# Expert rows fetched by indirect DMA and transposed, in place of one-hot products; gate and up weights in 4 KB runs

## The chip, the cores and the metric

One Trainium2 chip, one core of it. The metric is the device time of one execution of the whole program, in microseconds; lower is better.

## What is computed

The program is two layers behind each other on 512 tokens of width 1024, all in float32. The change lies in the expert part of the first layer, a mixture of 32 experts with 256 hidden columns each:

```python
h2 = rmsnorm(x, norm_ffn_g).reshape(b * s, d)
m = hierarchical_moe(h2, ...)
return x + m.reshape(b, s, d)

# hierarchical_moe, h is 512 x 1024
g_sel = argmax(group_logits)                       # one of 8 groups per token
top_vals, top_idx = lax.top_k(in_group, 2)         # two of the group's 4 experts
w_top = jax.nn.softmax(top_vals, axis=-1) * w_grp
combine = sum(one_hot(g_sel * 4 + top_idx, 32) * w_top[..., None], axis=1)
for e in range(32):
    hid = jax.nn.silu(h @ w_gate[e]) * (h @ w_up[e])   # 1024 -> 256
    out = out + (hid @ w_down[e]) * combine[:, e:e + 1]
```

Each token thus goes through two experts. The second layer (a convolution branch, a recurrent branch and a feed-forward part) is not touched.

## The kernel before

The whole first layer keeps its 512 rows `x` on the chip as 8 tiles of 128 x 512 (four blocks of 128 tokens, two halves of the width). Ahead of the experts, VectorE computes the routing from small logits (L763 to L841): per token and expert a position `pos` in the expert's list, and the combine weight `Cw`. An expert has 64 slots (`_CAP`); should any have more tokens, a loop under `tc.If(nmax > _CAP)` (L934) does the rest. With these inputs it is skipped.

The experts are worked off in 8 quads of four, and a quad in 2 pairs of two experts, so that a pair has 2 x 64 = 128 slots, one partition each. The order is:

- `onehots(qd)` (L811): VectorE compares slot numbers with `pos`: one 128 x 256 one-hot per block of tokens, slots of the quad's four experts along the columns.
- `gather(qd, oh)` (L858): the rows of a quad by products with the one-hots. Ahead of it, ScalarE and POOL or VectorE have split x into a rounded half `h2h` and a rest `h2l` (`halve`, L742 and L743). For each of 8 blocks of 128 features, four blocks of tokens times two halves are summed in PSUM: 64 matmuls of 128 x 256 (L867, L868). ScalarE (L870) and VectorE (L871) take the results out and scale them by the norm's gain. The result `xg` is already turned: features on partitions, slots along the columns.
- `pair(pr_, XG)` (L875): two 32-row products with a selector spread the positions and the weights over slots (L883, L887, L888); VectorE makes `oht` (L885), the one-hot with slots on partitions, and by two reductions (L890, L891) the scales `cw`. Then 64 matmuls with gate and up weights (L897), `Silu` on ScalarE (L900), the product with up and weight on VectorE (L901), two transposes (L904), their evacuation (`hT`, L153 or L155), 16 matmuls with the down weights (L912), and `split_t` of the result into halves `yph` (ScalarE, L159) and `ypl` (VectorE, L160).
- scatter, after both pairs of a quad: for each block of tokens and half of the width four matmuls with `oht` (L1021, L1022) and an addition to x (L1023). It is written under `tc.high_priority(offset=-200)`, which lets the scheduler put these 32 matmuls between the instructions of the next quad.

Weights come by `wexp` and `load_pair` (L719, L732) on SyncE's queue (L728): 12 tiles of 512 KB per pair, into a ring of 20 tiles (`NWE`). A tile of gate or up holds four blocks of 128 rows, row k x 128 + p on partition p, so each partition reads four runs of 256 numbers (1 KB); a down tile is one run of 1024 numbers (4 KB) per partition. The meta tokens of the second layer are prepared between the routing and the first quad (L999 to L1009); the tile `pmt` for their transposes is a PSUM tile of the tag `ms`.

The tile framework decides the order on each engine and the waits; every engine then works its list in order. PSUM tags have so many buffers: `xg` 1, `pg` 2, `py` 2, `ms` 1, `cb` 2. The scatter and its additions use `cb`; `oht`, `hd` and `hT` are tiles of the tag `T`.

The loop and the sizes that matter:

```python
PS.update({"xg": 1, "pg": 2, "py": 2, "ms": 1, "cb": 2})
for qd in range(8):
    XG = gather(qd, onehots(qd) if qd else oh0)
    YP = [pair(2 * qd + i, XG) for i in range(2)]
    with tc.high_priority(offset=-200):
        ...
```

## Time and profile before

| what | value |
|---|---|
| median of 3 runs | 2106.84 us (2103.09 to 2111.01) |
| the profiled execution | 2107.09 us, of it 2105.2 us in the span of the trace |
| mean granted TensorE clock | 0.987 of full speed |
| busy in the span | TensorE 96%, VectorE 64%, ScalarE 40%, POOL 1% |
| moved by DMA | 236.66 MB, 112 GB/s on average |

The expert stage lies at about 500 to 865 us of the span. A row of the trace names a line of the kernel, an engine, an operation and its tiles, output first. `PEld` is TensorE's load of the stationary operand, which overlaps the matmuls; `SPq` is SyncE's DMA queue. A line in a helper (L153, L155, L159, L160) stands for all that call it, so the tile's name tells which it is. In rows of the tables by stretch, `PEclk` is the granted clock as a share of full speed. A matmul's end is modelled, and consecutive matmuls overlap in the array.

### The profile page before, as it was taken

How to read it: one execution, taken by the hardware profiler on the slowest of the kernel's cores; microseconds unless marked ns; L12 is line 12 of the kernel's file. 1: busy time of each engine (PE TensorE's matmuls, PEld its weight loads, DVE VectorE, ACT ScalarE, POOL GpSimd, SP SyncE). 2: the span in 40 equal slices, each digit the busy share in tenths (PEclk: the TensorE clock that was granted, in tenths of full speed). 3: DMA queues.
4: the chain of work that ended last, by engine and by line, in shares of the span. 5: the costliest groups of instructions: out<-in, count | busy, mean ns of one | idle time of the engine just before them, and what ended most of it. 6: DMA issues, size and time to landing. Idle time of an engine off the chain costs nothing.

```text
span 2105.2 us, 42119 instructions
## 1 busy us (share of the span) xinstructions
PE 2018.8 (96%) x17517; PEld 1716.4 (82%) x17517; DVE 1340.9 (64%) x2937; ACT 842.2 (40%) x1741; POOL 23.9 (1%) x89
## 2 busy tenths in 40 slices
PE   7999999997999999899999999989999999999998
PEld 7778587886666666699888888878799989899997
DVE  4799835444434433879999889986443476455566
ACT  5443634332111111756655656544433253233333
POOL 0000000000000000100000000000000000000000
PEclk9999999998999999999999999989999999999999
DMA  5112021372799987321122212113443323332331
GB/s 159 56 31 82 21 80 41 100 258 68 251 313 326 307 289 253 53 79 54 40 57 57 56 42 57 53 42 102 151 124 97 107 61 92 97 93 90 91 116 51
DMA packets 282390, 236.66 MB, mean 112 GB/s; under 512 B 31500, under 2 KB 255795, under 8 KB 282195
## 3 DMA queue, kind: packets, MB, share of 16 engines
q1 hardware_dynamic: 282195, 233.92, 36.5%
q8 instruction: 140, 2.29, 0.5%
q14 instruction: 55, 0.45, 0.1%
HBM read 225.14 MB, written 8.74 MB: 111 GB/s over the span
## 4 chain that ended last, share of the span: by engine, by line
PE 61%; DVE 8%; ACT 4%; issue 1%; DMA 1%; SPq 0%; DVEq 0%; ACTq 0%
PE m L193 10%; PE m L191 10%; PE m L192 10%; PE ps L897 6%; PE ps L912 3%; DVE cv L1583 3%; PE ps L867 2%; PE q L191 2%; PE q L193 2%; PE q L192 2%; PE ps L868 1%; PE ps L1021 1%; PE ps L1022 1%; PE y L1522 1%; DVE wl L160 1%; PE x L1419 1%
## 5 line engine op out<-in xcount | busy, mean ns | idle before, releaser
L191 PE MATMUL m<-hh,wh 128*128 128x258 f32 (+1 forms) x1648 | 468.9, 290 | 7.9 <-ACT wh L159 3.0
L193 PE MATMUL m<-hh,wl 128*128 128x258 f32 (+1 forms) x1648 | 466.6, 290 | 3.4 <-DVE wl L160 2.1
L192 PE MATMUL m<-hl,wh 128*128 128x258 f32 (+1 forms) x1648 | 466.4, 289 | 2.4 <-DVE hl L160 1.7
L160 DVE TENSOR_TENSOR wl<-wr,wh 128x1024 fp32r<-128x1024 f32 (+1 forms) x205 | 248.0, 1212 | 227.7 <-ACT wh L159 224.7
L159 ACT ACTIVATE wh<-wr 128x1024 fp32r<-128x1024 f32 (+1 forms) x205 | 214.9, 1050 | 374.7 <-PE m L192 220.3
L191 PEld LDWEIGHTS m<-hh,wh 128*128 128x128 f32 x1648 | 308.3, 189 | 14.3 <-ACT wh L159 3.8
L193 PEld LDWEIGHTS m<-hh,wl 128*128 128x128 f32 x1648 | 307.7, 189 | 8.5 <-DVE wl L160 3.4
L192 PEld LDWEIGHTS m<-hl,wh 128*128 128x128 f32 x1648 | 308.5, 189 | 6.9 <-DVE hl L160 2.3
L1583 DVE SCALAR_TENSOR_TENSOR cv<-th,vec,cv 128x516 f32<-128x516 f32 (+9 forms) x240 | 176.5, 738 | 2.6
L897 PE MATMUL ps<-we,xg 128*64 128x256 f32 x1024 | 128.2, 386 | 0.6 <-ACT xg L870 0.6
L897 PEld LDWEIGHTS ps<-we,xg 128*64 128x64 f32 x1024 | 73.7, 137 | 42.4 <-issue 8.2
L191 PE MATMUL ps<-wh,hh 128*128 128x256 f32 x352 | 101.2, 288 | 1.1 <-ACT wh L159 0.9
L192 PE MATMUL ps<-wl,hh 128*128 128x256 f32 x352 | 100.7, 286 | 0.7 <-DVE wl L160 0.7
L193 PE MATMUL ps<-wh,hl 128*128 128x256 f32 x352 | 100.6, 286 | 0.0
L867 PE MATMUL ps<-oh,h2h 128*128 128x256 f32 x256 | 69.5, 300 | 0.0
L868 PE MATMUL ps<-oh,h2l 128*128 128x256 f32 x256 | 66.5, 288 | 2.7 <-PEq L934 2.7
L191 PEld LDWEIGHTS ps<-wh,hh 128*128 128x128 f32 x352 | 66.9, 190 | 2.3 <-ACT wh L159 1.3
L192 PEld LDWEIGHTS ps<-wl,hh 128*128 128x128 f32 x352 | 67.0, 190 | 1.5 <-DVE wl L160 1.0
L193 PEld LDWEIGHTS ps<-wh,hl 128*128 128x128 f32 x352 | 66.9, 190 | 0.4 <-DVE hl L167 0.2
L867 PEld LDWEIGHTS ps<-oh,h2h 128*128 128x128 f32 x256 | 50.2, 196 | 12.4 <-DVE ypl L160 5.7
L1790 ACT ACTIVATE uu<-m 128x258 f32<-128x258 f32 x88 | 33.2, 379 | 66.3 <-PE m L193 66.3
L912 PE MATMUL ps<-we,hT 128*64 128x512 f32 x256 | 58.1, 595 | 0.5 <-ACT hT L153 0.5
(565 smaller groups left out, 4356.3 us busy)
## 6 DMA issues: line engine op xcount, KB each, us to landing
wr<-in_w_in_dram SPq DMA_DIRECT2D x94, 512.0 KB
we<-in_w_gate_dram SPq DMA_DIRECT2D x64, 512.0 KB
we<-in_w_up_dram SPq DMA_DIRECT2D x64, 512.0 KB
we<-in_w_down_dram SPq DMA_DIRECT2D x64, 512.0 KB
wr<-in_ffn_up_dram SPq DMA_DIRECT2D x44, 512.0 KB
wr<-in_ffn_down_dram SPq DMA_DIRECT2D x18, 512.0 KB
wr<-in_w_out_dram SPq DMA_DIRECT2D x8, 512.0 KB
wr<-in_w_rwkv_out_dram SPq DMA_DIRECT2D x8, 512.0 KB
```

The lines of the kernel that those rows point to most:

```text
L159: A.activation(h, r, AF.Copy)
L160: V.tensor_tensor(l, r, h, op=OP.subtract)
L191: TE.matmul(o, lh, rh, start=start, stop=False)
L192: TE.matmul(o, lh, rl, start=False, stop=False)
L193: TE.matmul(o, ll, rh, start=False, stop=stop)
L867: TE.matmul(p[:, s * 256:(s + 1) * 256], H2H[b, k // 4][:, fs], oh[b], start=(b == 0), stop=False)
L868: TE.matmul(p[:, s * 256:(s + 1) * 256], H2L[b, k // 4][:, fs], oh[b], start=False, stop=(b == 3))
L897: TE.matmul(pg[s * 64:(s + 1) * 64, c0:c0 + 256], XG[k][:, o0 + s * 64:o0 + (s + 1) * 64], w[s][k], start=(k == 0), stop=(k == 7))
L912: TE.matmul(py[s * 64:(s + 1) * 64], hT[:, f * 128 + s * 64:f * 128 + (s + 1) * 64], wd[s][f][:, hf * 512:(hf + 1) * 512], start=(f == 0), ...
L1021: TE.matmul(p, oht[:, bs], yp[hf][0], start=(i == 0), stop=False)
L1583: V.scalar_tensor_tensor(cv[:, lo:], th[:, lo - d:N2 - d], cdw[:, f, 30 - d:31 - d], cv[:, lo:], op0=OP.mult, op1=OP.add)
L1790: A.activation(t, q, AF.Copy)
```

## The change

The rows of a pair's 128 slots are now fetched rather than computed.

- While x2, the input of the experts, is made, ScalarE's queue writes it to a DRAM tile `XD` (8 transfers of 256 KB). The splits of x into `h2h` and `h2l` are gone.
- A table `TB` holds per token its number, the norm's scale in two halves and the 32 combine weights in two halves. `gather` is now called per pair, and multiplies the one-hots of the pair with the table (4 matmuls of 128 x 68, new L851). Column 0 of the result is the token's number for each slot: VectorE casts it to an integer (`ix`, new L853), and POOL issues an indirect DMA that reads 128 rows of 4 KB (512 KB) from `XD` into `xr` (new L855, three buffers).
- `oht` comes from a comparison of the token number with a row of 0 to 511 (new L859), `cw` from four short additions and a product; the 32-row products and the reductions are gone.
- TensorE transposes the rows in 8 blocks of 128 x 128 in two groups of four (new L871), and VectorE takes each group out of PSUM, multiplied by the gain (new L873).
- `rows4`: gate and up tiles now hold 4 consecutive rows per partition, so that a partition reads one run of 4 KB. Feature p x 4 + k of a half belongs to block k, and the transposes take their columns in the same way.

The rest of `pair`, the scatter and the second layer are as before; their lines have moved (L897 is now L884, L900 is L887, L901 is L888, L904 is L891, L912 is L899, L1021 to L1023 are L1012 to L1014).

```diff
+    XD = tc.dram_tile([T1, D], F32, name="rows")
...
             logits(bp, c)
-            for b in range(2 * bp, 2 * bp + 2 * (c == 1)):
-                H2H[b, 0], H2L[b, 0] = (U("H", n_, F32R)[:, :512] for n_ in ("h2h", "h2l"))
-                halve(x2[b, 0][:, :512], H2H[b, 0], H2L[b, 0])
+            for b in range(2 * bp, 2 * bp + 2 * (c % 2)):
+                A.dma_start(XD[b * 128:(b + 1) * 128, (c // 2) * 512:(c // 2 + 1) * 512], x2[b, c // 2][:, :512])
...
     def load_pair(pr_):
         e = 2 * pr_
-        return ([[wexp(kview(w_g[e + s]), 4) for s in range(2)], [wexp(kview(w_u[e + s]), 4) for s in range(2)],
-                 [wexp(kview(w_d[e + s]), 1) for s in range(2)]])
+        def rows4(w):
+            return w.rearrange("(s p k) c -> s p k c", s=2, p=128)
+        return ([[sum((wexp(rows4(w[e + s])[i], 4) for i in range(2)), []) for s in range(2)] for w in (w_g, w_u)]
+                + [[wexp(kview(w_d[e + s]), 1) for s in range(2)]])
...
-    for b in range(4):
-        A.activation(H2H[b, 1], xv[b, 1], AF.Copy)
-        G.tensor_tensor(H2L[b, 1], xv[b, 1], H2H[b, 1], op=OP.subtract)
...
+    TB = u1.tile([128, 4, 68], F32R, name="tab")
+    V.tensor_copy(TB[:, :, 0::3][:, :, :2], C("tok")[:, :, None].to_broadcast([128, 4, 2]))
+    halve(rs4[:, :, None], TB[:, :, 1:2], TB[:, :, 2:3])
...
+    halve(Cw, TB[:, :, 4:36], TB[:, :, 36:68])
+    A.activation(warm, ex[:1, 0, :1], AF.Silu)
+
+    def gather(pr_, oh):
+
+        pt = ps("ms", n=68)
+        o0 = (pr_ % 2) * 128
+        for b in range(4):
+            TE.matmul(pt, oh[b][:, o0:o0 + 128], TB[:, b], start=(b == 0), stop=(b == 3))
+        ix = u1.tile([128, 1], I32, name="ix", bufs=4)
+        V.tensor_copy(ix, pt[:, 0:1])
+        xr = u1.tile([128, 1024], F32, name="xr", bufs=3)
+        G.indirect_dma_start(xr, None, XD[:, :], bass.IndirectOffsetOnAxis(ap=ix[:, :1], axis=0))
+        tb = u1.tile([128, 68], F32, name="tb", bufs=3)
+        A.activation(tb, pt, AF.Copy)
+        oht = U("T", "oht", F32R)
+        V.tensor_scalar(oht, C("iota"), tb[:, 0:1], None, op0=OP.is_equal)
...
         XG = []
-        for k2 in range(4):
-            p = ps("xg")
-            for s in range(2):
-                k = 2 * k2 + s
-                fs = slice((k % 4) * 128, (k % 4 + 1) * 128)
-                for b in range(4):
-                    TE.matmul(p[:, s * 256:(s + 1) * 256], H2H[b, k // 4][:, fs], oh[b], start=(b == 0), stop=False)
-                    TE.matmul(p[:, s * 256:(s + 1) * 256], H2L[b, k // 4][:, fs], oh[b], start=False, stop=(b == 3))
-            t = U("X", "xg")
-            A.activation(t[:, :256], p[:, :256], AF.Copy, scale=gff[:, 2 * k2:2 * k2 + 1])
-            V.tensor_scalar(t[:, 256:], p[:, 256:], gff[:, 2 * k2 + 1:2 * k2 + 2], None, op0=OP.mult)
-            XG += [t[:, :256], t[:, 256:]]
-        return XG
+        for s in range(2):
+            p = ps("xg").rearrange("p (k j) -> p k j", k=4)
+            xs = xr[:, 512 * s:512 * s + 512].rearrange("p (f k) -> p k f", k=4)
+            for k in range(4):
+                TE.transpose(p[:, k], xs[:, k], ident)
+            t = U("X", "xg").rearrange("p (k j) -> p k j", k=4)
+            V.tensor_tensor(t, p, gperm[:, s, :, None].to_broadcast([128, 4, 128]), op=OP.mult)
+            XG += [t[:, k] for k in range(4)]
+        return oht, cw, XG
...
     for qd in range(8):
-        XG = gather(qd, onehots(qd) if qd else oh0)
-        YP = [pair(2 * qd + i, XG) for i in range(2)]
+        oh = onehots(qd) if qd else oh0
+        YP = [pair(2 * qd + i, *gather(2 * qd + i, oh)) for i in range(2)]
```

How the order on the engines moves is shown at four places. The first is TensorE before, from the down products of one pair (L912) to those of the next: the three 32-row products lie among the gate and up products (L897), and behind the second pair's L912 the next quad's gather begins.

```order
L912 MATMUL ps<-we,hT 64x512 x8
L883 MATMUL ps<-posT,selp 128x512
L897 MATMUL ps<-we,xg 64x256 x5
L887 MATMUL ps<-cwT_5318,selp 128x512
L888 MATMUL ps<-cwT_5319,selp 128x512
L897 MATMUL ps<-we,xg 64x256 x12
L1021 MATMUL ps<-yph,oht 128x512
L1022 MATMUL ps<-ypl,oht 128x512
L1021 MATMUL ps<-yph,oht 128x512
L1022 MATMUL ps<-ypl,oht 128x512
L904 MATMUL ps<-cst_90,hd 128x128 x2
L912 MATMUL ps<-we,hT 64x512 x8
```

What these rows wait for are tiles that were loaded or made ahead; the gather (L867) needs only the one-hots and the halves of x.

The second place is TensorE after the change, at the second pair of a quad, with what each row waits for in brackets (DMASW is POOL's DMA). `tab` is the table, `xr` the fetched rows.

```order
L899 MATMUL ps<-we,hT 64x512 x4
L851 MATMUL ps<-tab,oh 128x68 [waits PE_49]
L851 MATMUL ps<-tab,oh 128x68 x3
L1012 MATMUL ps<-yph,oht 128x512
L1013 MATMUL ps<-ypl,oht 128x512
L1012 MATMUL ps<-yph,oht 128x512 [waits DVE_49,Activation_49]
L1013 MATMUL ps<-ypl,oht 128x512 [waits DVE_49]
L1012 MATMUL ps<-yph,oht 128x512 [waits DVE_49,Activation_49]
L1013 MATMUL ps<-ypl,oht 128x512
L871 MATMUL ps<-cst_90,xr 128x128 [waits DMASW3_49]
L871 MATMUL ps<-cst_90,xr 128x128 x3
L871 MATMUL ps<-cst_90,xr 128x128 [waits DVE_49]
```

The table's products now stand behind the down products of the pair ahead, and six scatter matmuls later come the transposes, which wait for the indirect DMA; the second four wait for VectorE, which empties the first group's PSUM buffer.

The third place is the same at the first pair of the next quad, from the ninth scatter matmul behind L851 on.

```order
L1012 MATMUL ps<-yph,oht 128x512 [waits DVE_49]
L1013 MATMUL ps<-ypl,oht 128x512
L1012 MATMUL ps<-yph,oht 128x512
L871 MATMUL ps<-cst_90,xr 128x128 [waits DMASW2_49]
L871 MATMUL ps<-cst_90,xr 128x128 x3
L1013 MATMUL ps<-ypl,oht 128x512
L1012 MATMUL ps<-yph,oht 128x512 [waits DVE_49]
L1013 MATMUL ps<-ypl,oht 128x512
L1012 MATMUL ps<-yph,oht 128x512
L871 MATMUL ps<-cst_90,xr 128x128 [waits DVE_49]
L871 MATMUL ps<-cst_90,xr 128x128 x3
```

Here eleven scatter matmuls stand between L851 and the first transposes, and four between the two groups.

The fourth is VectorE at the start of the stage: the end of the meta tokens (`mf`), then the first pair's index, its pair, and the second pair's index.

```order
L1000 TENSOR_SCALAR mf<-ps,vec_1326 128x16 x3
L853 CAST ix<-ps 128x1
L859 TENSOR_SCALAR oht<-cst_5230,tb 128x512
L861 TENSOR_TENSOR cw<-tb 128x1
L864 TENSOR_TENSOR cw<-tb 64x1 x2
L865 TENSOR_TENSOR cw<-cw 128x1
L873 TENSOR_TENSOR xg<-ps,gperm 128x512 x2
L888 SCALAR_TENSOR_TENSOR hd<-ps,cw,hd 128x256
L156 COPY hT<-ps 128x256
L161 TENSOR_TENSOR ypl<-ps,yph 128x512
L853 CAST ix<-ps 128x1
L161 TENSOR_TENSOR ypl<-ps,yph 128x512
```

The cast of the first index stands behind the last of the meta tokens, and that of the second pair between the two `ypl` of the first.

## Rows read from the trace of the kernel before

**Rows 1.** The page: busy time of each engine.
```profile
PE 2018.8 (96%) x17517; PEld 1716.4 (82%) x17517; DVE 1340.9 (64%) x2937; ACT 842.2 (40%) x1741; POOL 23.9 (1%) x89
```

**Rows 2.** Table by stretch, expert stage after its first pair: columns as its head says.
```profile
core 0: us, PE busy (x) PEld busy (x) DVE busy (x) ACT busy (x) POOL busy (x), PEclk, DMA share, GB/s
553.70:863.00 309.30, 306.10 (x1951) 193.95 (x1949) 132.56 (x302) 50.95 (x107) 3.86 (x8) 1.00 0.86 286
```

**Rows 3.** Waits of the engines, 540 to 845 us: total, times, longest us.
```profile
PEld ps L897 <- DMA we<-in_w_up_dram: 1.2, 5, 0.2
```

**Rows 4.** Waits of SyncE's DMA queue, 540 to 840 us.
```profile
SPq L728 <- PE ps L897: 104.7, 51, 6.7
```

**Rows 5.** Groups by line, 553.7 to 863 us: busy us, mean ns | idle before.
```profile
L867 PE MATMUL ps<-oh,h2h 128*128 128x256 f32 x224 | 58.6, 291 | 0.0
...
L868 PE MATMUL ps<-oh,h2l 128*128 128x256 f32 x224 | 56.4, 281 | 0.0
...
L1023 DVE TENSOR_TENSOR x<-ps,x 128x512 f32<-128x512 f32 x63 | 43.1, 688 | 20.7 <-PE ps L1022 19.7
...
L159 ACT ACTIVATE yph<-ps 128x512 fp32r<-128x512 f32 x31 | 18.4, 598 | 66.6 <-PE ps L1021 47.2 <-PE ps L912 18.6 <-PE ps L1022 0.4
...
L883 PE MATMUL ps<-posT,selp 32*128 32x512 f32 x15 | 7.4, 494 | 0.0
...
L901 DVE SCALAR_TENSOR_TENSOR hd<-ps,cw,hd 128x256 f32<-128x256 f32 x15 | 7.2, 483 | 54.2 <-ACT hd L900 54.2
...
L900 ACT ACTIVATE hd<-ps,cw 128x256 f32<-128x256 f32 x15 | 7.1, 475 | 118.2 <-PE ps L897 118.2
```

**Rows 6.** Timeline of TensorE, 649 to 652 us: start, duration, instruction [idle before].
```profile
649.09 0.28 PE L867 MATMUL ps<-oh,h2h 128*128 128x256 f32 x1
...
650.62 0.28 PE L868 MATMUL ps<-oh,h2l 128*128 128x256 f32 x1
...
650.83 0.50 PE L883 MATMUL ps<-posT,selp 32*128 32x512 f32 x1
...
651.25 0.44 PE L897 MATMUL ps<-we,xg 128*64 128x256 f32 x2
```

**Rows 7.** Timeline of TensorE, 114 and 482 to 484 us.
```profile
114.01 0.64 PE L498 MATMUL ps<-cst,tq 128*96 128x128 f32 x4 [0.69 <-ACT qaT L153]
...
482.35 1.08 PE L662 MATMUL ps<-wrt,x2T 128*128 128x40 f32 x8
...
483.25 0.37 PE L193 MATMUL ps<-wh,yl 128*128 128x256 f32 x1
```

**Rows 8.** Timeline of POOL and VectorE, 505 to 512 us.
```profile
505.38 3.98 POOL L743 TENSOR_TENSOR h2l<-x,h2h 128x512 fp32r<-128x512 f32 x3 [163.55 <-ACT h2h L742]
...
507.22 0.92 DVE L765 TENSOR_TENSOR ar<-lg,ar 128x32 f32<-128x32 f32 x1
...
511.83 0.18 DVE L765 TENSOR_TENSOR ar<-ar 128x16 f32<-128x16 f32 x1
```

**Rows 9.** Timeline, 0 to 9 and 523 to 527 us: DMA issues and first uses.
```profile
0.75 1.82 SPq L129 DMA_DIRECT2D xt<-in_x_dram  x4
...
4.67 0.63 ACT L253 ACTIVATE junk<-xt 128x512 f32<-128x512 f32 x1 [0.44 <-DMA xt<-in_x_dram]
...
7.49 0.63 ACT L253 ACTIVATE junk<-xt 128x512 f32<-128x512 f32 x1 [0.38 <-DMA xt<-in_x_dram]
...
523.60 1.60 SPq L999 DMA_DIRECT2D meta<-in_meta_tokens_dram  x2
...
526.02 0.67 DVE L1000 BATCH_NORM_STATS2 st<-meta 16x6 f32<-16x512 f32 x1
```

**Rows 10.** Timeline of TensorE, 549 to 556 us: a pair's down products.
```profile
550.23 3.60 PE L912 MATMUL ps<-we,hT 128*64 128x512 f32 x16
```

**Rows 11.** Table by stretch, three stretches around lowered clocks.
```profile
509.80:520.00 10.20, 5.05 (x22) 4.21 (x23) 7.35 (x39) 1.65 (x4) 1.24 (x1) 0.50 0.01 3
...
1120.80:1124.20 3.40, 1.83 (x20) 1.24 (x18) 3.40 (x13) 0.43 (x2) 0.00 (x0) 1.00 0.02 5
...
1124.20:1127.60 3.40, 3.40 (x42) 3.05 (x42) 2.67 (x6) 0.23 (x1) 0.00 (x0) 0.50 0.00 0
```

More of the change, by code (lines that the diff above doesn't have):

```diff
@@ L722, in wexp @@
         res = []
-        for k0 in range(0, 2048 // n, kt):
+        for k0 in range(0, src.shape[1], kt):
             wctr[0] = (wctr[0] + 1) % NWE
@@ L844, in tile_blocks @@
         dbg("Cw", Cw)
-    posT = u1.tile([32, 512], F32R, name="posT")
-    cwT = [u1.tile([32, 512], F32R, name=f"cwT{i}") for i in range(2)]
-    p = ps("cb")
-    for b in range(4):
-        TE.transpose(p[:32, b * 128:(b + 1) * 128], pos[:, b], ident)
-    A.activation(posT, p[:32], AF.Copy)
-    p = ps("cb")
-    for b in range(4):
-        TE.transpose(p[:32, b * 128:(b + 1) * 128], Cw[:, b], ident)
-    split_t(cwT[0], cwT[1], p[:32])
-    A.activation(warm, cwT[0][:1, :1], AF.Silu)
-    def gather(qd, oh):
-        XG = []
-        for k2 in range(4):
-            p = ps("xg")
-            for s in range(2):
-                k = 2 * k2 + s
-                fs = slice((k % 4) * 128, (k % 4 + 1) * 128)
-                for b in range(4):
-                    TE.matmul(p[:, s * 256:(s + 1) * 256], H2H[b, k // 4][:, fs], oh[b], start=(b == 0), stop=False)
-                    TE.matmul(p[:, s * 256:(s + 1) * 256], H2L[b, k // 4][:, fs], oh[b], start=False, stop=(b == 3))
-            t = U("X", "xg")
-            A.activation(t[:, :256], p[:, :256], AF.Copy, scale=gff[:, 2 * k2:2 * k2 + 1])
-            V.tensor_scalar(t[:, 256:], p[:, 256:], gff[:, 2 * k2 + 1:2 * k2 + 2], None, op0=OP.mult)
-            XG += [t[:, :256], t[:, 256:]]
-        return XG
@@ new lines, in tile_blocks @@
+    A.activation(warm, ex[:1, 0, :1], AF.Silu)
[12 more added lines that the diff above has]
+        V.tensor_scalar(oht, C("iota"), tb[:, 0:1], None, op0=OP.is_equal)
+        cw = sm.tile([128, 2], F32, name="cw", bufs=4)
+        V.tensor_tensor(cw[:, 0:1], tb[:, 1:2], tb[:, 2:3], op=OP.add)
+        for s in range(2):
+            hs, e = slice(64 * s, 64 * s + 64), 4 + 2 * pr_ + s
+            V.tensor_tensor(cw[hs, 1:2], tb[hs, e:e + 1], tb[hs, e + 32:e + 33], op=OP.add)
+        V.tensor_tensor(cw[:, 1:2], cw[:, 0:1], cw[:, 1:2], op=OP.mult)
+        XG = []
+        for s in range(2):
+            p = ps("xg").rearrange("p (k j) -> p k j", k=4)
[6 more added lines that the diff above has]
+        return oht, cw, XG
@@ L893, in pair @@
+    def pair(pr_, oht, cw, XG):
+        wg, wu, wd = load_pair(pr_) if pr_ else first
         pg = ps("pg")
@@ L896, in pair @@
                 for s in range(2):
-                    TE.matmul(pg[s * 64:(s + 1) * 64, c0:c0 + 256], XG[k][:, o0 + s * 64:o0 + (s + 1) * 64],
+                    TE.matmul(pg[s * 64:(s + 1) * 64, c0:c0 + 256], XG[k][:, s * 64:(s + 1) * 64],
                               w[s][k], start=(k == 0), stop=(k == 7))
@@ L934, in tile_blocks @@
     with tc.If(nmax > _CAP):
+        xp = {}
+        for b in range(4):
+            for s in range(2):
+                xp[b, s] = U("A", "xp")
+                SY.dma_start(xp[b, s], XD[b * 128:(b + 1) * 128, s * 512:(s + 1) * 512])
         with tc.For_i(0, E_, 1) as ei:
@@ L956, in tile_blocks @@
                     for b in range(4):
-                        TE.matmul(p, H2H[b, k // 4][:, fs].bitcast(F32), oh[:, b], start=(b == 0), stop=False)
-                        TE.matmul(p, H2L[b, k // 4][:, fs].bitcast(F32), oh[:, b], start=False, stop=(b == 3))
+                        TE.matmul(p, xp[b, k // 4][:, fs], oh[:, b], start=(b == 0), stop=(b == 3))
                     xg = U("T", "fx", n=128)
```

32 lines of the change are left out of this document (6 added, 26 removed).

## The prediction

> **What bounds the kernel now.** The page comes first. TensorE is busy for 96% of the span and no other engine for more than 64% [rows 1], so a change counts by what it does to TensorE's stream. The change touches the expert stage, and the table by stretch says how full that stream is there. From 553.7 us, where the first pair of experts is done, to 863 us, where the last one ends, TensorE is busy for 306.10 of 309.30 us at a clock of 1.00 of full speed (the 2.4 GHz level) [rows 2]. That is 15 pairs of 20.6 us. The DMA engines are busy for 0.86 of the same time, which looks like a second limit, so the waits are read next. The longest of TensorE's waits for weight tiles sums to 1.2 us in five waits [rows 3]. The queue that loads the weights waited 104.7 us, in 51 waits, for TensorE to be done with gate and up buffers [rows 4]. So the weights are early and the stage runs at TensorE's pace. The **4 KB runs** of gate and up are therefore costed at nothing: what hides them is the lead that the ring of 20 tiles already has.
>
> **What is removed.** The one-hot gather issued 224 + 224 matmuls (L867, L868) in the stage and each pair three 32-row ones (L883, L887, L888), 45 in all [rows 5]. A matmul's duration includes its way through the array, so the price is the distance between starts. From 649.09 to 650.62 us there are 13 steps, 0.118 us each, and 448 × 0.118 = 52.9 us. An L883 holds the stream from 650.83 to 651.25, 0.42 us, and 45 × 0.42 = 18.9 us [rows 6]. Together **−71.8 us**. The splits into halves, the evacuations at L870/L871 and the two reductions per pair (L890, L891) were on ScalarE and VectorE beside this and are worth nothing by themselves.
>
> **What is added to TensorE.** Per pair eight transposes (new L871) and four small products of one-hots with the table (new L851). Four transposes of this size took 0.64 us [rows 7], in which the last one's way through the array is counted (0.28, as in [rows 6]); that is three steps in 0.36, and I take 0.12 each: 120 × 0.12 = 14.4 us. Eight products 40 columns wide went from 482.35 to 483.25, 0.113 each [rows 7]: 60 × 0.113 = 6.8 us. Together +21.2, and the stream's own balance is **−50.6 us**.
>
> **What is added as waiting.** Here the order decides. Before, the rows of the next four experts needed nothing that was not already on the chip, and they filled the stream while a pair's results went through ScalarE and VectorE. Now each pair's index comes from L851, which stands right behind the down products of the pair ahead, and the transposes that need the gathered rows stand six scatter matmuls later (second pair of a quad) or eleven later (first pair). TensorE takes its instructions in order, so the gate products behind L871 wait as well. On VectorE the cast of the index stands between the two ypl splits of the pair ahead, so the second split, and the scatter of that half, waits for L851 too. The weight queue is not behind the gather, which has POOL's own queue, and POOL has eight operations besides in the whole stage [rows 2].
>
> How long from the end of the down products to the rows' landing? L851 takes 4 × 0.113 = 0.45, its result appears about 0.28 later (the duration of one matmul, [rows 6]), and the cast to an index is a short VectorE operation, 0.18 for such [rows 8]: 0.95 with rounding. POOL's part, making the descriptors, is in no row. It can't be under nothing, and its longest operation, a full tile pass, was 3.98/3 = 1.33 [rows 8]; it makes 128 addresses and no pass over 512 columns, so I take 0.65. The transfer is 512 KB. The shortest near it is 32 KB of meta tokens, issued at 523.60 and used at 526.02: 2.4 us. The nearest in size are the first loads of the kernel: issued from 0.75, the first 256 KB were used at 3.50, the second at 4.67, the fourth at 7.49 [rows 9]. Two tiles in an empty queue are thus 3.9 us, four 6.7. The gather meets the weight queue just when TensorE has freed tiles, so it lies between two and four; I take 3.9 + 0.5. So **W = 0.95 + 0.65 + 4.4 = 6.0 us**, with ends 0.95 + 0 + 2.4 = 3.4 and 0.95 + 1.33 + 6.7 = 9.0.
>
> Against this stand fillers. A 512-column matmul takes 0.22 of the stream (16 in 3.60 us, [rows 10]). For a quad's second pair: 0.45 + 6 × 0.22 = 1.8 us. For its first pair: 0.45 + 11 × 0.22 = 2.9, and the first of them wait for yph and ypl of the last half (0.598, and 0.69 as any VectorE pass over 512 columns of PSUM, L1023, [rows 5]), so 3.4. The second pair has also lost the work that hid its own chain: between its two groups of transposes stands the VectorE pass that empties their single PSUM buffer (0.69 + 0.2 of hand-overs, which I put at 0.1 each), behind its gate and up products Silu and the multiply (0.475 + 0.483 + 0.3, that is 1.3, [rows 5]) and then the evacuation of hT (256 columns as for Silu, 0.475 + 0.2): 2.8 us. In the first pair 4, 7 and 4 scatter matmuls lie in these three places (0.9, 1.5 and 0.9 us) and hide them. So a second pair waits 6.0 − 1.8 + 2.8 = 7.0 us, eight times: 56. A first pair waits 6.0 − 3.4 = 2.6, seven times: 18.2. Together **+74.2**, and with the balance above +23.6 us.
>
> **The clock.** A wait also costs behind its end. The granted clock stood at 0.50 (1.2 GHz) from 509.8 to 520 with TensorE idle for half of it, and from 1124.2 to 1127.6 at 0.50, behind a stretch at 1.00 in which it was busy 1.83 of 3.4 us [rows 11]. The waits forecast are of the same size as these. A stretch of 3.4 us at half rate gives up 1.7 us of work. The second pairs' waits should all lead to one, the shorter ones of the first pairs for the most part: 13 × 1.7 = **+22.1 us**. The Trainium skill, "TensorE: Matmul & The Clock Gate", section "HAM oscillation — how this bites in real kernels", tells of a kernel whose TensorE waited for a transfer ahead of each tile and had its clock lowered each time; by that the loss would come at all 15 waits and the time be 2156 us; the rows above agree as far as they go.
>
> **The start of the stage** I put at nothing. The routing chain on VectorE loses POOL's subtraction beside it: L765 took 0.92 us while it ran and, on half the columns, 0.18 after it [rows 8]; with two more like it some 3 us. The first gather gives that back, since its cast now stands on VectorE behind the whole chain of the meta tokens. The table of rows in DRAM is written by eight transfers that ScalarE issues, in place of splits that cost it more; pair 1's weights are issued later, at the time of the meta tokens (523.60, [rows 9]), but have until some 553 us.
>
> **Sum.** −71.8 + 21.2 + 74.2 + 22.1 = +45.7. The profiled execution took 2107.09 us, 0.25 above the median of 2106.84, so the same term goes on the median: **2152 us**.
>
> **Rivals.**
> (a) *Waits as forecast, full clock*: the scatter matmuls break the waits up, so that no lowered stretch follows. For it: in the expert stage before, the clock never fell. Against it: it fell behind a stretch with 1.83 of 3.4 us busy [rows 11]. −50.6 + 74.2: 2130 us.
> (b) *The gather is quicker and the two sides cancel.* If index to landing takes 3.2 us, POOL's part included, midway between the 2.4 of the meta tokens and the 3.9 of two tiles [rows 9], W is 4.15; a second pair waits 2.35 + 2.8 = 5.15 × 8 = 41, a first 0.75 × 7 = 5; −50.6 + 46 = −4, and a few lowered stretches bring it above nothing: 2102 to 2115. The rows speak against it, with 3.9 for these bytes in an empty queue. The Trainium skill, "DMA: Bandwidth & Descriptors", section "Anatomy of one DMA — SWDGE (gpsimd) path", gives 2.0 us plus the bytes at 436 GB/s, an estimate of 3.2 us for 512 KB; by that rule this case is the one.
> (c) *Faster: the gather is done in 2.4 us*, because its 128 rows go over all DMA engines ahead of the weights. W is 3.4; a second pair waits 1.6 + 2.8 = 4.4 × 8 = 35, a first pair not at all, the clock holds: −50.6 + 35 = −16, 2091 us. It decides from the point where all waits are under 40 us, W about 3.8. For it: a small load that quick is in the trace [rows 9]. It can't be much faster: 6.8 MB per pair in 19.6 us are 347 GB/s, and 286 in 0.86 of the engines' time [rows 2] are 333 with all of it, so the longer runs must carry some per cent more for this case, and nearly all would be used.
> (d) *The change's second half does nothing*: taken as certain above, since its transfers are waited for by nobody.
>
> **How the numbers follow.** Forecast 0.48; (a) 0.17; (b) 0.15; (c) 0.20. Half a per cent is 10.5 us, about what a measurement of this kernel can tell from no change. Slower by more than that holds the forecast and (a), 0.65; within it (b), 0.15; faster (c), 0.20. The forecast's own range is 2125 to 2200: its upper end is W = 9.0, second pairs 10.0 × 8, first pairs 5.6 × 7, all 15 lowered stretches: −50.6 + 119.2 + 25.5 = +94, 2201. Below, the range takes in (a), (b) and half of (c): **2090 to 2200**.
>
> **What would show it.** In the new profile, right: TensorE waits for the gathered tile ahead of L871 in nearly every pair, some 4 us in second pairs and 2 to 3 in first ones; the clock row shows 6 to 9 tenths in the slices of the expert stage; the stage is about 355 us long where it was 309; the weight queue still waits for TensorE. A wait for Silu or hT of about 1 us each in second pairs. Wrong: a clock of 1.00 in the stage (then (a)), waits at L871 under 2 us (then (b) or (c)), or TensorE waiting for weight tiles.

## The result and the profile after

| kernel | median us | runs | ratio to before |
|---|---|---|---|
| before | 2104.98 | 2103.09 to 2111.01 | |
| changed | **2210.07** | 2207.39 to 2214.14 | 1.0496 [1.0467, 1.0524] |

Slower, as the likeliest case had it, but by 105 us where 45.7 were forecast; the time lies above the range's end of 2200. The profiled execution has a span of 2212.4 us, 107.2 above before's 2105.2. The page of the changed kernel: busy times, TensorE's busy tenths in 40 slices, and the granted clock in the same slices.

```profile
PE 2000.7 (90%) x17133; PEld 1683.0 (76%) x17133; DVE 1322.6 (60%) x2919; ACT 829.0 (37%) x1719; POOL 33.9 (2%) x101
...
PE   7999999994677777779999999998899999999998
...
PEclk9999999996789888889999999998999999999999
```

TensorE is busy for 18 us less than in [rows 1], and the kernel is 107 us longer. The low digits of the busy row (4 to 7) and of the clock row (6 to 8, with one 9 among them) stand in the same slices, the expert stage. The table by stretch has the changed kernel's stage behind its first pair, 563.3 to 970.7 us, and three pieces of it, each of two pairs; its columns are those of [rows 2].

```profile
563.30:970.70 407.40, 299.05 (x1668) 170.17 (x1666) 121.05 (x286) 39.98 (x87) 20.91 (x31) 0.86 0.63 236
...
667.80:719.70 51.90, 37.81 (x221) 21.88 (x220) 15.19 (x36) 4.17 (x9) 1.87 (x2) 0.90 0.69 261
719.70:773.50 53.80, 40.70 (x221) 23.21 (x220) 15.22 (x36) 4.17 (x9) 1.87 (x2) 0.81 0.68 254
773.50:827.30 53.80, 40.45 (x221) 22.69 (x220) 15.25 (x36) 4.18 (x9) 1.87 (x2) 0.84 0.66 254
```

The same table of the kernel before, for two of its pairs:

```profile
667.10:708.00 40.90, 40.90 (x268) 26.19 (x266) 16.82 (x37) 5.51 (x11) 0.00 (x0) 1.00 0.92 307
```

The stage takes 407.4 us where [rows 2] has 309.3: 98.1 of the 107.2. A further 9.6 us have passed before the stage's second pair begins (563.3 in place of 553.7), and 0.5 are won back behind the stage. In the stage TensorE stands for 407.40 − 299.05 = 108.4 us, where it stood for 3.2. So waiting is +105, and the busy time has shrunk by 7 alone, though two pairs have 47 matmuls less: the lowered clock gives most of that back. The waits of TensorE in this stretch (total, times, longest us):

```profile
PE ps L871 <- DMA xr<-rows,ix: 68.5, 15, 7.5
PE ps L1012 <- DVE cw L865: 10.1, 7, 1.4
PE ps L1012 <- DVE x L1014: 9.0, 10, 1.8
PE ps L891 <- DVE hd L888: 9.0, 8, 1.1
PE ps L871 <- DVE xg L873: 6.3, 8, 0.8
PE ps L899 <- ACT hT L154: 3.8, 8, 0.5
PE ps L1013 <- DVE ypl L161: 1.0, 6, 0.2
```

The first row is the gather itself, in all 15 pairs. Rows two and three are for the most part scatter matmuls in the gather's shadow, which come late as well (2.6 us of row three lie behind the last pair, and as much was there before). The profile names cw (L865) as what row two waits for, but L1012 reads yph and oht and not cw. By the kernel it needs the PSUM buffer that the addition to x (L1014) empties; in these seven cases it starts 0.15 us behind the end of that addition, and VectorE comes to it only behind oht and three additions for cw, which are made from the same table product as the index. The next three rows are the chain of a second pair, which has no filler left. No weight tile appears. The weight queue in turn waits for TensorE, 256 us of 470 where [rows 4] had 105 of 300 (waits of SyncE's queue, 520 to 990 us):

```profile
SPq L727 <- PE ps L884: 256.2, 58, 19.5
```

One pair by the timeline (start, duration, instruction, idle before), all engines, rows left out:

```profile
692.96 3.66 PE L899 MATMUL ps<-we,hT 128*64 128x512 f32 x16 [0.47 <-ACT hT L154]
...
695.78 1.75 SPq L727 DMA_DIRECT2D we<-in_w_up_dram  x4
...
696.54 0.63 PE L851 MATMUL ps<-tab,oh 128*128 128x68 f32 x4
...
697.21 0.16 DVE L853 CAST ix<-ps 128x1 int32<-128x1 f32 x1 [0.93 <-PE ps L851]
...
697.64 0.94 POOL L855 DMA_INDIRECT xr<-rows,ix  x1 [24.23 <-DVE ix L853]
...
701.02 0.40 PE L1012 MATMUL ps<-yph,oht 128*128 128x512 f32 x1
...
706.31 1.13 PE L871 MATMUL ps<-cst,xr 128*128 128x128 f32 x4 [4.89 <-DMA xr<-rows,ix]
```

From the end of the down products (696.54, where L851 starts) to the first transpose 9.8 us pass: 1.1 to POOL's start, the rest until the rows are there. The last filler ends at 701.4. POOL's own part is 0.94. And the four transposes behind the wait take 1.13 us where four took 0.64 at the full clock [rows 7] (the same transposes take 0.63 in `e9_fill2` below, at a clock of 1.00). Over all 16 gathers the view of the gathered tile gives, from POOL's issue to landing:

```profile
DMA to landing us min/median/max: 4.2/7.7/10.0
```

The one of 4.2 is the last gather, at 938.8 us, when no packet of weights is under way any more; the first takes 4.9. In the packet records, a gather between these two sends its first packet 4.15 us behind POOL's start (median; the first gather 1.83, the last 1.64) and its packets go over in 3.3 (2.76 and 2.25).

### The profile page after: what moved, and what is told of

Same layout as the page of the kernel before. It is cut to its first block, busy times and chain, and to the rows that moved or that the text cites. A ratio compares the mean times of both kernels' runs of the same rounds, so it can differ in the third digit from the quotient of the medians.

```text
span 2212.4 us, 41353 instructions
## 1 busy us (share of the span) xinstructions
PE 2000.7 (90%) x17133; PEld 1683.0 (76%) x17133; DVE 1322.6 (60%) x2919; ACT 829.0 (37%) x1719; POOL 33.9 (2%) x101
## 4 chain that ended last, share of the span: by engine, by line
PE 45%; issue 17%; DVE 8%; ACT 4%; DMA 1%; POOL 1%; SPq 0%; DVEq 0%; POOLq 0%; ACTq 0%
PE m L194 10%; PE m L192 10%; PE m L193 10%; DVE cv L1574 2%; PE q L192 2%; PE q L194 1%; PE q L193 1%; PE y L1513 1%; PE x L1410 1%; DVE wl L161 1%; PE ps L884 1%; PE x L1493 1%; PE x L1482 1%; ACT wh L160 1%; PE m L1603 1%
## 5 line engine op out<-in xcount | busy, mean ns | idle before, releaser
L884 PE MATMUL ps<-we,xg 128*64 128x256 f32 x1024 | 133.9, 427 | 0.0
L884 PEld LDWEIGHTS ps<-we,xg 128*64 128x64 f32 x1024 | 80.2, 156 | 51.5 <-issue 21.8
L887 ACT ACTIVATE hd<-ps,cw 128x256 f32<-128x256 f32 x16 | 7.6, 474 | 290.2 <-PE ps L884 290.2
L871 PE MATMUL ps<-cst,xr 128*128 128x128 f32 x128 | 34.2, 417 | 80.9 <-DMA xr<-rows,ix 73.9
L871 PEld LDWEIGHTS ps<-cst,xr 128*128 128x128 f32 x128 | 23.5, 217 | 93.7 <-DMA xr<-rows,ix 81.2
L873 DVE TENSOR_TENSOR xg<-ps,gperm 128x512 f32<-128x512 f32 x32 | 22.1, 692 | 115.2 <-PE ps L871 115.2
L1014 DVE TENSOR_TENSOR x<-ps,x 128x512 f32<-128x512 f32 x64 | 43.7, 687 | 57.7 <-PE ps L1013 56.9
L1012 PE MATMUL ps<-yph,oht 128*128 128x512 f32 x128 | 59.4, 464 | 19.7 <-DVE cw L865 10.1
```

The source lines that it names most:

```text
L871: TE.transpose(p[:, k], xs[:, k], ident)
L884: TE.matmul(pg[s * 64:(s + 1) * 64, c0:c0 + 256], XG[k][:, s * 64:(s + 1) * 64], w[s][k], start=(k == 0), stop=(k == 7))
L1012: TE.matmul(p, oht[:, bs], yp[hf][0], start=(i == 0), stop=False)
L1014: V.tensor_tensor(xv[b, hf], p, xv[b, hf], op=OP.add)
```

## The experiments

**Theory:** the gather lies on TensorE's path, and its transfer is slow because it shares the DMA engines with the weights; the clock follows from the waits. **Rivals:** the gather is slow by itself; the longer runs of the weights, not the index, are what costs; the lowered clock alone makes the difference.

### The gather without company, and among shorter runs

`e2_quiet` uses pair 0's weights for all pairs, so no weight moves in the stage (and its results are those of other experts); `e3_run1k` is the changed kernel with the weights read in runs of 1 KB as before.

```diff
 # e2_quiet
-        wg, wu, wd = load_pair(pr_) if pr_ else first
+        wg, wu, wd = first
 # e3_run1k (and the order of features in gperm and in the transposes)
-        return ([[sum((wexp(rows4(w[e + s])[i], 4) for i in range(2)), []) for s in range(2)] for w in (w_g, w_u)]
-                + [[wexp(kview(w_d[e + s]), 1) for s in range(2)]])
+        return ([[wexp(kview(w_g[e + s]), 4) for s in range(2)], [wexp(kview(w_u[e + s]), 4) for s in range(2)],
+                 [wexp(kview(w_d[e + s]), 1) for s in range(2)]])
```

> All pairs use the weight tiles of pair 0, so no weights are loaded after them (the output is then that of wrong experts). This leaves the indirect DMA alone on the DMA engines. Theory (the gather is late because it starts behind the weight tiles queued on each DMA engine, 4.3 us from POOL's issue to the first packet where it was 1.8 for the first gather, and then shares the engines): from issue to landing 4.6 us as for the first gather instead of 7.7, the wait per pair 3 us shorter, the time 2140 to 2165 us. Rival (the latency belongs to the indirect DMA itself): issue to landing stays above 7 us and the time above 2195.

> The changed kernel with gate and up weights read in runs of 1 KB again, the transposes and the gain set back to match. Theory (weights are early in both kernels, the run length does nothing by itself): within 1% of the changed kernel, 2190 to 2230 us; a small gain is possible, since a packet of the gather then alternates with short packets. Rival (the 4 KB runs carry weights faster and that shortens the waits): slower by more than 20 us, TensorE waiting for weight tiles.

Issue to landing, first in the kernel without weight loads, then in the one with 1 KB runs:

```profile
DMA to landing us min/median/max: 4.3/4.5/4.8
```

```profile
DMA to landing us min/median/max: 4.3/7.1/8.9
```

Alone, a gather takes 4.3 to 4.8 us, and the kernel 2150.55 (one run), 60 us less than the changed kernel. This falls in the theory's range; that the gather is as slow by itself is out. Company costs 3.2 us per gather. By the packet records most of it, 2.5 us, passes before the first packet (1.64 us alone), the rest while the packets go over (2.5 alone). That the gather's packets stand behind weight packets which the DMA engines already hold would fit this, but no run shows it. With 1 KB runs the first packet comes later still, at 4.64, but the packets go over in 1.9 us in place of 3.3; the gather lands at 7.1, and the kernel takes 2197.37 (1.044 [1.0422, 1.0457]), 13 us less than with 4 KB. So in the changed kernel the 4 KB runs are no help but a small harm.

### The index and the fetch taken off the path

`e1_ahead2` computes index and fetch two pairs ahead and leaves the transposes in their place in the program (oht gets another buffer, since it now lives longer):

```diff
     def gather(pr_, oh):
...
-        oht = U("T", "oht", F32R)
+        oht = U("A", "oht", F32R)
...
+        return xr, oht, cw
+
+    def turn(xr):
...
+            while len(got) < min(p_ + AHEAD + 1, 16):
...
+                got.append(gather(n_, ohs[n_ // 2]))
+            xr, oht, cw = got[p_]
+            YP.append(pair(p_, oht, cw, turn(xr)))
```

> The table products, the index and the indirect DMA of a pair are issued two pairs ahead of its transposes; nothing else is changed but the buffers that this needs. Theory (the wait from index to landing, 9.8 us per pair in the changed kernel, stands on TensorE's path and its clock falls behind each wait): TensorE's waits for the fetched rows go from 74 us to under 10, the clock in the stage from 0.86 to above 0.97, and the time falls from 2210 to 2065 to 2090 us, below the kernel before, because TensorE's stream is 50 us shorter. Rival 1 (what was lost is the work that hid a pair's own chain through Silu, hT and the single PSUM buffer): the waits for the rows go, waits for ScalarE and VectorE take their place, and the time stays above 2150. Rival 2 (the DMA engines are the bound, with 6.8 MB per pair): TensorE waits for weight tiles instead, 15 pairs of 21 us, about 2110.

2102.56 us (2099.32 to 2104.85), ratio 0.9976 [0.9965, 0.9988]. The gather's wait is gone but for 9.2 us, and with it the whole loss of 105 us; that it was the gather's place is shown. TensorE's order changes with it, though: the framework now has rows turned two to three pairs ahead (by the starts in the trace), so that other pairs' products stand in a pair's chain. What is shown is the fetch ahead together with the order that comes of it. And the time is 12 us over the upper end of what was expected from the work removed. Waits of TensorE, 520 to 990 us, and the table by stretch of this kernel:

```profile
PE ps L875 <- DMA xr<-rows,ix: 9.2, 5, 2.4
```

```profile
580.00:620.00 40.00, 40.00 (x244) 22.73 (x240) 17.12 (x40) 4.56 (x10) 1.87 (x2) 1.00 1.03 409
...
680.00:740.00 60.00, 54.19 (x337) 32.28 (x334) 24.51 (x55) 5.26 (x12) 2.81 (x3) 1.00 0.90 334
```

In its first part both are full, TensorE (40.00 of 40 us) and the DMA engines (409 GB/s at a share of 1.03); later TensorE stands for a tenth of the time.

`e11_ahead3` fetches three pairs ahead and makes the first two gathers before the meta tokens are handled; `e5_ahead3w` also issues pair 1's gate and up loads at the start of the stage, before the branch; `e6_ahead3w1k` is `e5_ahead3w` with 1 KB runs.

```diff
 # e11_ahead3, against e1_ahead2
+    got = [gather(0, oh0), gather(1, oh0)]
     mt = [U("T", "meta")[:16] for _ in range(2)]
...
+            XG = turn(xr)
+            ahead(p_ + 3)
+            YP.append(pair(p_, oht, cw, XG))
 # e5_ahead3w, in addition
-    first = load_pair(0)
+    first = [load_pair(0), load_pair(1, False)]
```

> As e1, with the index and the fetch three pairs ahead, the first two fetches written ahead of the preparation of the meta tokens, and gate and up weights of pair 1 loaded ahead of the branch. In e1 TensorE still waited 9 us for rows, the stage began 7 us late and the weight queue then ran at 409 GB/s with nothing in hand. Theory (only the place of the gather was wrong; the arithmetic saved is real): the start of the stage is back, no waits for rows, a pair takes 17 to 18 us, bounded about equally by TensorE's stream (20.6 less 3.4 us) and by 6.8 MB at 409 GB/s (16.6 us), and the time is 2050 to 2075 us. Rival (TensorE's stream got no shorter in fact, because the work that hid the chain of a pair is gone): 2090 us or more, with waits for ScalarE and VectorE in the place of those for rows.

> e5 with gate and up weights in runs of 1 KB again. Theory (run length matters only where the DMA engines bind, and they bind in e5): the rate of the weights falls from 409 towards 320 GB/s, a pair takes about 21 us, and the time is 2100 to 2125 us, 40 us or so above e5, with TensorE waiting for weight tiles. Rival (run length never matters): within 10 us of e5.

> e5 without the early weights of pair 1: fetch three pairs ahead, two of them ahead of the meta tokens. In e5 the first gather met 4 MB of pair 1's weights on the DMA engines, first packet 4.3 us after POOL's issue, and VectorE then stood for 9 us ahead of the first oht; pair 0's down products started at 560.5. Theory (the DMA engines bind e5: 100 MB of weights at up to 409 GB/s from 510 us on leave little): the start is 8 us earlier, but the weights of pair 1 come as much later, and the time is as in e5, 2080 to 2092 us. Rival (the start is worth its time): 2070 to 2080 us.

| kernel | us | ratio |
|---|---|---|
| e11_ahead3 | 2092.37 (2090.55 to 2095.47) | 0.9938 [0.9921, 0.9955] |
| e5_ahead3w | 2088.64 (2086.29 to 2091.38) | 0.9913 [0.9888, 0.9937] |
| e6_ahead3w1k | 2086.8 (2085.29 to 2089.22) | 0.99 [0.9877, 0.9924] |

All three beat both kernels, the one before by 1% or less; between the last two no difference is to be seen. `e11_ahead3` lies 0.4 us over the upper end of what was expected; pair 0's down products start 8.6 us earlier than in `e5_ahead3w` (551.8 in place of 560.5), and the time is 4 us longer. `e5_ahead3w` missed its 2050 to 2075. Its table by stretch: two stretches of 120 us, then two pieces of two pairs each.

```profile
560.00:680.00 120.00, 119.61 (x766) 70.03 (x763) 52.18 (x126) 15.94 (x35) 6.89 (x8) 1.00 1.02 401
680.00:800.00 120.00, 108.22 (x663) 63.19 (x663) 42.83 (x96) 11.53 (x25) 4.35 (x5) 1.00 0.94 342
...
695.80:737.00 41.20, 37.09 (x225) 21.68 (x224) 15.40 (x36) 3.96 (x9) 1.87 (x2) 1.00 0.89 328
737.00:777.90 40.90, 35.86 (x223) 21.11 (x223) 14.40 (x35) 3.96 (x9) 1.87 (x2) 1.00 0.93 332
```

For the first 120 us the DMA engines carry 401 GB/s at a share of 1.02, and TensorE stands for 0.4 us. In this part the saved work shows: from 560.5 to 674.9 us, the starts of L903 in the trace, a pair takes 16.4 us where it took 20.6 (a little of this is scatter put off until later). After that two pairs still take 41 us, as before the change, with 36.5 busy and the clock at 1.00. The waits there, of TensorE and then of the weight queue (563 to 850 us):

```profile
PE ps L1032 <- DVE x L1034: 4.7, 8, 1.4
PE ps L875 <- DMA xr<-rows,ix: 2.8, 2, 1.5
PE ps L895 <- DVE hd L892: 2.7, 4, 1.1
PE ps L895 <- DMA we<-in_w_gate_dram: 2.2, 2, 1.1
PE ps L903 <- ACT hT L154: 1.9, 4, 0.5
```

```profile
SPq L727 <- PE ps L888: 70.4, 37, 5.5
SPq L727 <- PE ps L903: 42.6, 22, 5.3
SPq L727 <- DMA we<-in_w_gate_dram: 24.6, 23, 2.0
```

TensorE waits for the buffers of the scatter (x), for two late fetches and for a pair's own chain (hd, hT). The fourth row names a weight tile, but L895 turns hd and reads no weights, so it belongs to the chain. No matmul with weights waits for them, and the weight queue waits mostly for TensorE. For the most part these are the waits that the rival on record for `e5_ahead3w` names, though the time lies 1.4 us under its 2090: with the gather products gone, too little stands in these places. A limit by the weights is not shown, and `e6_ahead3w1k` speaks against it: its stretch 680 to 800 us stands at a share of 1.07 with 369 GB/s, where `e5_ahead3w` has 0.94, and its time is the same. This also refutes the idea that the longer runs carry the gain; the 40 us expected of the theory did not come, the rival was right.

### What the clock costs

Idle matmuls ahead of the transposes keep TensorE busy in the wait: constants times constants, nothing of the result changes.

```diff
+            with tc.high_priority(offset=-400):
+                for _ in range((9 if pr_ % 2 else 6) if s == 0 and pr_ else 0):
+                    TE.matmul(p, ident, cfill, start=True, stop=True)
```

`e8_fill` has 38 and 8 of them (second, first pairs of a quad) in place of 9 and 6, `e9_fill2` 19 and 6; `e12_fill3` is the one shown.

> The changed kernel with idle matmuls put in between the table products and the transposes: 8 of 512 columns ahead of a quad's first pair, where the scheduler then puts all scatter matmuls as well, and 38 ahead of its second pair, about as long as the wait of 9.8 us. They write a PSUM buffer that the transposes overwrite. The waits stay, but TensorE is busy in them. Theory (43 us of the loss are the clock lowered behind each wait): the granted clock in the stage goes from 0.86 to 0.97 or more, L884 comes back from 427 to about 386 ns, and the time falls to 2165 to 2195 us although 46 matmuls per quad are added. Rival (the lowered clock costs nothing, since the weights or the waits set the pace): 2205 us or more.

> e8 again with the idle matmuls that e8 should have had: one float32 matmul of the program turned out to be two of 0.22 us in the trace, so e8's filled wait was twice the gather's. Now 19 in the program (8.4 us) ahead of a quad's second pair, and 6 beside the scatter ahead of its first. Theory (43 us of the loss are the lowered clock): a pair takes 24 to 25 us where it took 27, the clock in the stage is above 0.96, and the time 2160 to 2190 us. Rival (the lowered clock costs nothing): 2205 us or more.

> e9 again, with 9 idle matmuls of the program instead of 19 ahead of a quad's second pair: each of them, with 128 stationary columns, took 0.86 us, not 0.44, so e9's wait was 15.4 us there. In the first pairs e9 was as meant: TensorE busy through the wait, the clock 1.00 in the whole stage, and 12.1 us from the first transpose to the down products, where the changed kernel needs 13.9. Theory: the lowered clock costs what it adds to that stretch, 1.8 us in each pair, 27 us in all; a pair takes 24 to 25.5 us and the time is 2175 to 2190 us. Rival (the clock costs nothing on the path): 2205 us or more.

`e8_fill`: 2379.43 us (one run), mis-sized: a float32 matmul in the program is two instructions in the trace here, 0.43 us from start to start, so the filler outlasted the gather by far. `e9_fill2`: 2241.15 (one run), still too much in second pairs, 30.9 us each, but first pairs take 25.6. `e12_fill3`: 2198.55 (2197.26 to 2199.83), ratio 1.0437 [1.0383, 1.0492], over the 2175 to 2190 expected. The stage's table in `e9_fill2`, then in `e12_fill3`:

```profile
580.00:900.00 320.00, 311.37 (x1561) 168.46 (x1558) 89.76 (x201) 24.24 (x52) 10.31 (x11) 1.00 0.66 246
```

```profile
580.00:900.00 320.00, 297.71 (x1522) 161.56 (x1522) 95.16 (x215) 26.45 (x57) 11.27 (x12) 0.96 0.70 264
```

With TensorE busy through the wait the clock stays at 1.00. Then the path from a pair's first transpose to its down products takes 12.1 us (first pairs of `e12_fill3`, both kinds of `e9_fill2`, from the starts of these lines in the trace), where the changed kernel takes 13.9. For second pairs, with the same instructions in both, that is the clock: 1.8 us. In first pairs the fillers have also moved 15 scatter matmuls out of this stretch; there `e2_quiet`, which has the changed kernel's order, is the fairer measure, with a clock of 1.00 and 12.4 us in first pairs from the second quad on. So an estimate is 8 × 1.8 + 7 × 1.6 = 25 us over 15 pairs. In `e12_fill3` second pairs still wait for the gather and take 14.0 us, and only some 12 us come back.

### The start of the stage

`e10_startm` makes pair 0's gather before the meta tokens are handled.

```diff
+    g0 = gather(0, oh0)
     mt = [U("T", "meta")[:16] for _ in range(2)]
...
-        YP = [pair(2 * qd + i, *gather(2 * qd + i, oh)) for i in range(2)]
+        YP = [pair(2 * qd + i, *(gather(2 * qd + i, oh) if qd + i else g0)) for i in range(2)]
```

> The changed kernel with the first pair's gather alone written ahead of the preparation of the meta tokens. In the changed kernel pair 0's down products start at 557.1 us where they did at 550.2, and end 9.5 us later. Theory (the first gather waits on VectorE behind the whole chain of the meta tokens, and all is pushed back by it): the start is 8 to 12 us earlier, the rest is unchanged, 2197 to 2204 us. Rival (the start is set by the weights of pair 0 or 1, or by the lowered clock): within 4 us of the changed kernel, 2206 to 2214.

The timeline of the changed kernel at this place, and that of `e10_startm`:

```profile
529.02 0.28 PE L999 MATMUL ps<-cst,meta 16*128 16x16 f32 x1 [15.23 <-DVE meta L996]
...
534.49 1.04 PE L851 MATMUL ps<-tab,oh 128*128 128x68 f32 x4 [0.48 <-DVE mf L1000]
...
540.94 1.13 PE L871 MATMUL ps<-cst,xr 128*128 128x128 f32 x4 [5.41 <-DMA xr<-rows,ix]
```

```profile
522.62 1.04 PE L851 MATMUL ps<-tab,oh 128*128 128x68 f32 x4 [8.66 <-DVEq L921]
...
531.70 1.13 PE L871 MATMUL ps<-cst,xr 128*128 128x128 f32 x4 [8.05 <-DMA xr<-rows,ix]
```

In the changed kernel the first index stands behind the meta tokens, ahead of whose first product TensorE stands for 15 us, and the gather comes behind that. Before, gather products filled this time. Moved ahead, the first transpose comes 9.2 us sooner, the down products of pair 0 at 551.1 in place of 557.1 and those of the last pair at 948.7 in place of 956.0. So 6 to 7 us are kept, and some 3 are lost again in pair 0, between whose products the eight for the meta tokens now stand. The kernel takes 2205.48 (2203.05 to 2207.29), ratio 1.047 [1.0452, 1.0487]: 4.6 us less by the medians and 6.9 by the profiled spans, under the 8 to 12 expected and over the rival's 4.

### The longer runs alone

`e4_b4k` is the kernel before with the 4 KB runs. The features then come in another order, and the one-hot products pick every fourth column of the halves. `e7_b4kc` stores the halves in the new order instead, so that the products read 128 columns side by side.

```diff
 # e4_b4k
-                fs = slice((k % 4) * 128, (k % 4 + 1) * 128)
+                fs = slice(k % 4, 512, 4)
 # e7_b4kc, against e4_b4k
-                halve(x2[b, 0][:, :512], H2H[b, 0], H2L[b, 0])
+                halve(*(t_.rearrange(r_, k=4) for t_, r_ in ((x2[b, 0][:, :512], "p (f k) -> p k f"), ...
+                fs = slice((k % 4) * 128, (k % 4 + 1) * 128)
```

> The kernel before with gate and up weights in runs of 4 KB, and nothing of the gather: the one-hot products take every fourth column of x so that features agree. Theory: no change, 2105 us within 0.5%; the DMA share of the stage falls from 0.86 and the weight queue waits longer for TensorE. Rival 1 (weights bind somewhere): faster by 10 us or more. Rival 2 (the strided stationary operand costs TensorE time): slower by 10 us or more, with longer weight loads at the gather's lines.

> The kernel before with weights in runs of 4 KB, as e4, but with the halves of x stored in permuted order when they are split, so that the stationary operand of the one-hot products is contiguous again. In e4 the weight load at those lines took 0.325 us where it took 0.189 before, 448 of them, and the time rose by 48 us. Theory: this is the whole of e4's loss, and the runs by themselves change nothing: 2105 us within 0.5%. Rival (4 KB runs cost or give something where TensorE binds): over 10 us away.

`e4_b4k`: 2154.23, ratio 1.0231 [1.0214, 1.0248]. `e7_b4kc`: 2109.52 (2106.03 to 2111.47), 1.0008 [0.9998, 1.0019]. The longer runs do lower the DMA share of the stage, from the 0.86 of [rows 2] to 0.77 (553 to 863 us of `e7_b4kc`):

```profile
553.00:863.00 310.00, 306.82 (x1957) 193.70 (x1954) 132.73 (x301) 50.95 (x107) 3.84 (x8) 1.00 0.77 287
```

TensorE's weight loads for these products in `e4_b4k`, then in `e7_b4kc` (busy us, mean ns, idle before):

```profile
L872 PEld LDWEIGHTS ps<-oh,h2l 128*128 128x128 f32 x224 | 72.7, 325 | 0.0
```

```profile
L874 PEld LDWEIGHTS ps<-oh,h2l 128*128 128x128 f32 x224 | 42.3, 189 | 0.8
```

The loss of `e4_b4k`, 48 us against 2106.7 for the kernel before beside it, is not the DMA's. A weight load of every fourth column takes 0.325 us in place of 0.189, and the median distance from one product's start to the next is 0.234 in place of 0.120. With the columns side by side the 4 KB runs alone change nothing.

## Why the prediction was wrong, and where it was right

Three kernels split the 107.2 us. Two pairs keep TensorE busy for 40.9 us before, for a mean of 39.7 in the changed kernel's three pieces at clocks of 0.81 to 0.90, and for 36.5 in `e5_ahead3w`'s two pieces, which have the changed kernel's instructions at 1.00. With 7.5 such pieces in the stage:

| term | forecast | measured |
|---|---|---|
| removed and added work | −50.6 | (36.5 − 40.9) × 7.5 = −33 |
| waiting | +74.2 | +105 |
| clock | +22.1 | (39.7 − 36.5) × 7.5 = +24 (25 by the paths) |
| start of the stage | 0 | +9.6 |
| sum | +45.7 | about +106, of 107.2 |

**Bound and direction: right.** TensorE's order set the pace; the removed arithmetic was on the path, but so was the gather that took its place.

**Waiting: mechanism right, mis-sized.** The step that failed is "I take 3.9 + 0.5". POOL's part of 0.65 and the 3.9 add up to 4.55 us, and the gather alone measured 4.5; in `e2_quiet` it is 5.4 to 6.0 us from the table product to the transposes (starts in the trace), as W = 6.0 has it. Half a microsecond for the weights' company was the error; it is 3.2. In the changed kernel the same way takes 8.1 to 11.1 us, 9.2 in the mean of 14 pairs, and 5.4 in the last, which meets no weights. The upper end of the range had 9.0 for it. That the time lies above the range is due to work and start, which the range held fixed. By parts: the waits for the gather and in its shadow are 68.5 + 10.1 + 6.4 = 85.0 where 51.8 had been put; the chain without fillers is 9.0 + 6.3 + 3.8 = 19.1 where 2.8 × 8 = 22.4 had been put. The scatter matmuls were counted as fillers in full, though VectorE's work on the table product holds up one of them in 14 of the 15 pairs.

**Removed and added work: mis-sized by some 18 us.** The removed instructions were priced a little low: in two pairs of before, the distances from their starts to the next ones sum to 8.2 us for the gather products and 2.35 for the 32-row ones, and seven gathers and 15 pairs make 75 where 71.8 had been put. What failed is the step "the stream's own balance is −50.6 us", which lets all other instructions follow each other as tightly as they had. In `e5_ahead3w`'s two pieces, at the full clock, two pairs' 32 scatter matmuls take 9.0 us where they took 7.7 (to the next start, or to a matmul's own end where a wait follows), gate and up 15.7 where they took 15.0, and transposes and table products 3.4 where 2.8 had been put. With 0.2 for the others that is 2.8 us per two pairs, 21 in the stage, less the 3 above. So the missing 18 us are found by line. Why these matmuls stand further apart stays open; a part of it is the way of a matmul through the array (0.28 us in [rows 6]), which counts as busy time ahead of a wait.

**Clock: right in cause, and in size partly by luck.** The waits led to lowered stretches, and with TensorE kept busy in them the clock stood at 1.00. But a mean of 0.86 over 407.4 us is an estimate of 114 us at the lower level, where 13 × 3.4 = 44 had been put; part of the 114 lies in the waits themselves and costs nothing. The section "HAM oscillation — how this bites in real kernels" of the Trainium skill's "TensorE: Matmul & The Clock Gate", by which the loss comes at every wait, agrees with the changed kernel: from the first transpose to the down products the mean clock was 0.72 to 0.89 in all 15 pairs. In `e2_quiet`, where the waits are shorter, it was 1.00 in first pairs from the second quad on and 0.76 to 0.80 in second ones. Rival (a), waits at a full clock, is out.

**Start: put at nothing, it was 9.6 us.** The step counted what VectorE loses and gains; it did not ask what TensorE does while the meta tokens are handled. Before, gather products filled that stretch; now the first index waits behind its end. Moving it ahead gave back 4.6 to 6.9 us (`e10_startm`); the rest was not followed.

**Rivals (b) and (c)** needed a gather of 3.2 and 2.4 us. The rule of the Trainium skill's "DMA: Bandwidth & Descriptors", "Anatomy of one DMA — SWDGE (gpsimd) path", gives an estimate of 3.2 for these bytes; measured were 4.5 alone and 7.7 among the weights, so that the measurement decides against it. **(d)**, "taken as certain", holds for the runs alone (1.0008) but not beside the gather: nobody waits for the weights, but the gather meets them, and there the 4 KB runs cost 13 us.

Taking the gather off the path turns +5% into −0.6% (`e11_ahead3`, three pairs ahead) and −0.9% (`e5_ahead3w`, with pair 1's weights loaded early as well). No kernel tried got more: in the middle of the stage a pair takes 20.6 us again, 18.2 busy, and the rest goes into the chain, the scatter's buffers and late fetches.

## What to carry to other kernels

A fetch by an index that the kernel has just computed is a chain of its own (product, cast, descriptors, transfer): issue it pairs ahead, or it costs its whole length at every step, and the clock behind it. Price such a transfer in the company in which it will run: beside a full weight queue it took 7.7 us, alone 4.5. And before arithmetic is removed, ask which waits it filled: they come back even where the gather is out of the way.

## What the runs showed that was not expected

- A small transfer beside busy queues loses most of its time before its first packet (2.5 of 3.2 us). With 1 KB weight packets in place of 4 KB ones its first packet went out 0.5 us later (4.64), and it still landed 0.6 us sooner.
- A weight load of every fourth float32 column takes 0.325 us where 128 columns side by side take 0.189, and that alone made a kernel 2.3% slower.
- A plain float32 matmul of 128 × 128 by 512 columns appears as two instructions, 0.43 us from start to start.
- 365 to 369 GB/s in runs of 1 KB at a DMA share of 1.06 to 1.07, and 401 and then 342 GB/s in runs of 4 KB at 1.02 and 0.94, gave the same time (`e6_ahead3w1k`, `e5_ahead3w`).
